# The first two modulation vectors of layer 0 from column slabs, with the projection of x two tiles behind

## The chip, the cores and the metric

The kernel runs on one core of a Trainium2 chip. The metric is the device time of one execution in microseconds (us). A core has a matrix engine (PE; the loading of its stationary operand is shown as PEld), a vector engine (DVE), an activation engine (ACT), GpSimd (POOL), a queue that issues most DMAs (SP), and 16 DMA engines that all queues share. Each engine works its instructions off in the order in which the build put them, and waits where an instruction's inputs are not there yet.

## The reference

A two-layer transformer block on x (512 tokens x 1024) with a context (256 tokens x 1024). Each layer is modulated by six vectors of 1024 that come from a matrix product with the conditioning vectors; the first two of layer 0 (shift `sh1`, scale `sc1`) are what the first projection waits for. Everything is float32.

```
mod  = silu(c)     @ ada_w[l] + ada_b[l]        # 1024 -> 6 * 1024
modc = silu(c_ctx) @ ada_w[l] + ada_b[l]
sh1, sc1, g1, sh2, sc2, g2 = split(mod, 6)      # likewise csh1 ... of modc
a  = rmsnorm(h,  norm1_g[l]) * (1 + sc1)  + sh1
ac = rmsnorm(hc, norm1_g[l]) * (1 + csc1) + csh1
y, yc = even_mixer(a, ac, ...)   # layer 0: q, k, v, u projections, attention, gated MLP
h = h + g1 * y ; h = h + g2 * swiglu(modulate(h, ...)) ; the same for hc ; then layer 1
```

## The kernel before

All activations are kept transposed: tile k of x (`hx[k]`) holds features 128k to 128k+127 in the partitions and the 512 tokens in the columns; there are 8 tiles. A float32 product is done as three matmuls (`mm3`, lines 100 to 102): each operand is split into a rounded part (hi) and a rest (lo), and hi x hi, hi x lo and lo x hi are summed in PSUM. For a weight block (`unit`) the raw block is loaded by SP (line 72), ACT makes hi (line 75), POOL makes lo (line 78). There are five raw buffers, and six weight slots plus three of a tag `wq`.

The start of `even()` is what the change is about. In the kernel before it goes like this:

- x (2 MB) is loaded in four pieces. ACT squares each tile and DVE adds the squares up (`squares`, lines 185 and 187); a matmul with ones sums over partitions (line 150), DVE makes 1/rms (lines 129 to 133) and a diagonal of it (line 167), and a matmul with ones (`spread`, line 177) puts 1/rms of each token in all partitions of a PSUM bank.
- The modulation vectors: `ada_load` (line 344) loads two row blocks of one vector's 1024 columns in 1 MB, into four buffers (tag `ar`). `ada_step` (line 351) multiplies the 32-column conditioning block `cst[:, k, :]` with row block k, four column quarters into four partition groups of one PSUM bank; the sum over all eight row blocks must be complete before any of the vector is known. `ada_out` copies the bank to SBUF (line 358), transposes it (line 360) and adds the bias and the gain (lines 364 and 368). The scale is done first, then the shift: 4 MB of weights each.
- `warm` (line 376) puts matmuls without use between the steps, two behind each step of the scale, three behind each step of the shift and six at the end.
- When the scale is there, DVE multiplies all eight tiles by scale and 1/rms (line 394). When the shift is there, ACT adds it and makes hi (line 457), DVE makes lo (line 458). Only then do the x products of the first half of the q and k columns begin: for each tile k, four column groups n, 96 matmuls of 512 columns in all into two PSUM pairs (`pw`).
- Then `modulate` does the same for the context tiles (lines 193 to 195), and the context products (96 matmuls of 256 columns, into `pb`) follow; `evacuate` (line 437) copies the x products out, and `rope` (lines 245 to 248, DVE and POOL) rotates them.
- The four other vectors of layer 0 (`ada_ahead`, `ada_some`, 16 loads of 1 MB, two vectors together) go between the products until well into the v projection.

The second half of the q and k columns, the v projection, attention and the rest of the kernel come behind that. The order within an engine's queue is fixed by a scheduler at build time, with priorities from the program's order; `issue_after` holds a load back until another DMA has been issued.

Of the kernel before, what the change touches and what calls it, by code (L numbers as in the profile page):

```python
# [14 lines left out]
P = 128  # L15
D = 1024
# [10 lines left out]
class Builder:  # L27
# [286 lines left out]
    def even(self):  # L314
        tc, nc, a = self.tc, self.nc, self.a
        self.open_ring(512, 5, 6)
        self.adap = tc.alloc_tile_pool(name="ada0", bufs=1, side="left", reuse_waits="tile")
        self.ropep = tc.alloc_tile_pool(name="rope0", bufs=1, side="left", reuse_waits="tile")
# [13 lines left out]
        self.ident = self.load(p0, a["ident"], [P, P], "ident")  # L332
# [6 lines left out]
        def ada_load(j, n, k):  # L339

            m = 2 // n
            t = self.adap.tile([P, m, n * D], F32, name=self.uid("ar"), tag="ar", bufs=4)
            src = a["ada0"][k * P:(k + m) * P, j * D:(j + n) * D].rearrange("(k p) c -> p k c", p=P)
            self.last_slab = nc.sync.dma_start(t, src)
            return [t[:, i, :] for i in range(m)]
# [8 lines left out]
        def ada_out(j, n, ps, pt):  # L354

            row = self.tmp("t")
            nb = 2 * n
            nc.scalar.copy(row[:, :nb * P], ps[:, :nb * P])
            for b in range(nb):
                nc.tensor.transpose(pt[:, b * P:(b + 1) * P], row[:, b * P:(b + 1) * P], self.ident)  # L360
            v = pt[:, :nb * P].rearrange("p (b q w) -> p q b w", b=nb, q=4)
            q = lambda t: t[:, j * KT:(j + n) * KT].rearrange("p (q b) -> p q b", q=4)
            for who in range(2):
                nc.vector.tensor_tensor(q(self.mod[who]), v[:, :, :, who], q(self.adab), ALU.add)
                for i in range(j, j + n):
                    if i in (1, 4):
                        m = self.mod[who][:, i * KT:(i + 1) * KT]
                        nc.vector.scalar_tensor_tensor(m, m, 1.0, self.gain(i // 3, 0), ALU.add, ALU.mult)
            return row
# [9 lines left out]
        slabs = sum([ada_load(1, 1, k) for k in range(0, KT, 2)], [])  # L379
        self.adab = self.load(p0, a["ada_b"], [P, 96], "adab")  # L380
        self.gains = self.load(p0, a["gains"], [P, 5 * KT], "gains")
        rd = self.rstd_diag([(sq, TX)], 1.0 / D)[0]
        ps0 = self.fill()
        for k in range(KT):
            ada_step(ps0, k, slabs[k])
            if k % 2:
                slabs += ada_load(0, 1, k - 1)
            if k == 3:
                rx = self.spread(rd)
            warm(slabs[k][:, :P], 2)  # L390
        scaled = self.bank()
        ada_out(1, 1, ps0, scaled)
        for k in range(KT):
            nc.vector.scalar_tensor_tensor(hx[k], hx[k], self.modcol(0, 1, k, 0), rx, ALU.mult, ALU.mult)
        ps0 = self.fill()
        for k in range(KT):
            ada_step(ps0, k, slabs[KT + k])
# [11 lines left out]
        def ada_ahead(n):  # L409
            for _ in range(min(n, len(rest))):  # L410
                j, k = rest.pop(0)
                loaded.append((j, k, ada_load(j, 2, k)[0]))
# [26 lines left out]
        with tc.issue_after(self.last_slab.ins):  # L439
            ctx_load()  # L440
        for half, heads in enumerate(((0, 1), (2, 3))):
            w2 = [self.wide(), self.wide()]
            accx = [w[:, h * 512:(h + 1) * 512] for w in w2 for h in range(2)]
            W = []
            for k in range(KT):
                t = self.adap.tile([P, 2, 512], F32R, name=self.uid("wq"), tag="wq", bufs=3) if k % 3 == 2 else None
                with tc.issue_after(self.last_slab.ins) if half == 0 else ExitStack():
                    W.append(self.blocks(a["qk"][half, k], 512, t=t))
                    if half == 0:
                        if k > 4:  # L450
                            with tc.issue_after(self.last_w.ins):
                                ada_ahead(1)
                        if k == 7:
                            tabs += [self.load(self.ropep, a[n], [P, TX], n) for n in ("cos", "sin")]
                if half == 0:
                    t, sh = hx[k], self.modcol(0, 0, k, 0)
                    nc.scalar.activation(axx[k][0], t, AF.Identity, bias=sh)
                    nc.vector.scalar_tensor_tensor(axx[k][1], t, sh, axx[k][0].bitcast(F32), ALU.add, ALU.subtract)  # L458
                elif k % 2:
                    ada_ahead(1)  # L460
                    ada_some()
                for n in range(4):
                    self.mm3(accx[n], W[k][n], axx[k], k == 0, k == KT - 1)
                if half == 0 and k == 4:
                    rd = self.rstd_diag([(self.squares(hc, TC), TC)], 1.0 / D)[0]
                if half == 0 and k == 5:
                    rc = self.spread(rd)
                    for i in range(KT):
                        self.modulate(hc[i], TC, self.modcol(0, 1, i, 1), self.modcol(0, 0, i, 1), rc, axc[i])
# [863 lines left out]
def prep(inp):  # L1333
# [12 lines left out]
    r["ada0"] = c(A["ada_w"][0])  # L1346
# [57 lines left out]
```

## Time and profile before

| what | value |
|---|---|
| runs of the kernel before | 1641.31, 1640.96, 1637.72 us; median 1640.96 |
| the profiled execution, first to last instruction (its span) | 1641.9 us |
| PE busy, share of the span | 1542.8 us, 94% |
| DVE, ACT, POOL busy | 65%, 44%, 47% |
| DMA queue of SP, share of 16 engines | 28.4% |
| mean granted clock of PE | 0.977 |

The page gives for the profiled execution its span alone; a time of its own beside it is not listed. The span lies 0.6 to 4.2 us above the three runs. A row of the timeline reads: start in us, duration, engine, line, operation, output<-inputs, shapes, count, and in brackets how long the engine sat idle before and what released it. A row of the windows reads: from:to, length, busy time (and instructions) of PE, PEld, DVE, ACT and POOL, the granted clock of PE, the busy share of the DMA engines, and GB/s.

### The profile page before, as it was taken

To read this page: it belongs to the slowest core of one execution; us is meant where nothing else is said; L and a number is where in the kernel's file an instruction comes from. 1 tells how busy PE (TensorE), PEld (TensorE's weight loads), DVE (VectorE), ACT (ScalarE), POOL (GpSimd) and SP (SyncE) were. 2 spreads that over 40 slices of the span, in tenths; PEclk is the share of its full clock that TensorE was granted. 3 is DMA by queue.
4 is the path that set the end of the run, shared out by engine and by line. 5 is a ranking of instruction groups with operands and counts; after the bars stand their busy time and mean duration, and the time that the engine had idled before them with its cause. 6 is when DMAs were issued, how large, how long until landed. Compare 5 with 4: busy or idle time off the path is not lost.

```text
span 1641.9 us, 24642 instructions
## 1 busy us (share of the span) xinstructions
PE 1542.8 (94%) x9547; PEld 1367.1 (83%) x9547; DVE 1073.0 (65%) x1980; ACT 724.5 (44%) x1472; POOL 766.9 (47%) x543
## 2 busy tenths in 40 slices
PE   6999989999999999999999988999989999999996
PEld 4776877899899889998989978777868989898886
DVE  4621788756857788666665585665667857666665
ACT  2423675645533233333333244555664544444443
POOL 0463221062157666666666316532222466675662
PEclk9999989999999999999999999999999999999998
DMA  8744100141223343343432012110233222322201
GB/s 317 298 153 169 40 7 1 65 139 68 76 79 116 105 139 131 105 150 126 142 131 77 27 51 91 52 33 25 74 116 123 65 103 92 101 90 103 90 27 52
DMA packets 47957, 161.98 MB, mean 99 GB/s; under 512 B 5472, under 2 KB 9952, under 8 KB 40160
## 3 DMA queue, kind: packets, MB, share of 16 engines
q1 hardware_dynamic: 47696, 160.28, 28.4%
q8 instruction: 75, 1.23, 0.3%
q14 instruction: 42, 0.34, 0.1%
q10 hardware_dynamic: 144, 0.13, 0.0%
HBM read 158.29 MB, written 2.10 MB: 98 GB/s over the span
## 4 chain that ended last, share of the span: by engine, by line
PE 69%; DVE 11%; POOL 6%; DMA 5%; ACT 4%; issue 3%; POOLq 0%; SPq 0%; DVEq 0%; ACTq 0%
PE pw L100 9%; PE pw L101 9%; PE pw L102 9%; PE pb L100 7%; PE pb L101 7%; PE pb L102 7%; POOL w L917 5%; DMA raw<-ffn_in 3%; PE pf L100 3%; PE pf L101 2%; PE pf L102 2%; PE pb L1257 2%; PE pb L1246 2%; PE pf L351 2%; DVE t L968 2%
## 5 line engine op out<-in xcount | busy, mean ns | idle before, releaser
L100 PE MATMUL pw<-ax,w 128*128 128x384 f32 (+2 forms) x732 | 237.5, 328 | 16.1 <-DVE q L1012 6.7
L101 PE MATMUL pw<-ax,w 128*128 128x384 f32 (+2 forms) x732 | 237.9, 325 | 4.1 <-DVE ax L458 2.5
L78 POOL TENSOR_TENSOR w<-raw,w 128x512 fp32r<-128x512 f32 (+1 forms) x84 | 127.6, 1526 | 243.2 <-ACT w L75 220.8
L102 PE MATMUL pw<-ax,w 128*128 128x384 f32 (+2 forms) x732 | 236.7, 325 | 2.1 <-POOL w L917 2.1
L917 POOL TENSOR_TENSOR w<-raw,w 128x512 fp32r<-128x512 f32 x119 | 177.7, 1507 | 54.2 <-ACT w L913 53.4
L917 POOL TENSOR_TENSOR w<-t,w 128x512 fp32r<-128x512 f32 x90 | 133.4, 1482 | 139.9 <-ACT w L913 136.5
L100 PE MATMUL pb<-hh,w 128*128 128x512 f32 x480 | 167.3, 362 | 12.8 <-ACT hh L116 8.3
L766 DVE SCALAR_TENSOR_TENSOR xT<-pb,mod,xT 128x512 f32<-128x512 f32 (+3 forms) x208 | 144.5, 704 | 43.8 <-PE pb L102 43.1
L101 PE MATMUL pb<-hh,w 128*128 128x512 f32 x480 | 171.2, 358 | 0.5 <-POOL hh L117 0.5
L102 PE MATMUL pb<-hh,w 128*128 128x512 f32 x480 | 170.7, 357 | 0.0
L100 PEld LDWEIGHTS pw<-ax,w 128*128 128x128 f32 x732 | 142.0, 195 | 27.2 <-DVE q L1012 8.1
L100 PE MATMUL pw<-T,w 128*128 128x384 f32 (+1 forms) x508 | 159.1, 314 | 4.8 <-DVE hs L1008 2.4
L101 PE MATMUL pw<-T,w 128*128 128x384 f32 (+1 forms) x508 | 158.6, 312 | 4.0 <-DVE T L117 4.0
L102 PE MATMUL pw<-T,w 128*128 128x384 f32 (+1 forms) x508 | 158.2, 312 | 0.0
L101 PEld LDWEIGHTS pw<-ax,w 128*128 128x128 f32 x732 | 142.6, 195 | 12.1 <-DVE ax L458 3.4
L102 PEld LDWEIGHTS pw<-ax,w 128*128 128x128 f32 x732 | 142.4, 195 | 6.0 <-POOL w L917 2.7
L913 ACT CAST w<-t 128x512 fp32r<-128x512 f32 x104 | 64.5, 621 | 176.8 <-DVE t L968 122.5
L917 POOL TENSOR_TENSOR w<-rawo,w 128x512 fp32r<-128x512 f32 x63 | 94.1, 1493 | 66.5 <-ACT w L913 66.5
L100 PEld LDWEIGHTS pb<-hh,w 128*128 128x128 f32 x480 | 89.5, 189 | 27.0 <-ACT hh L116 10.8
L100 PEld LDWEIGHTS pw<-T,w 128*128 128x128 f32 x508 | 97.2, 192 | 9.7 <-DVE hs L1008 3.9
L101 PEld LDWEIGHTS pw<-T,w 128*128 128x128 f32 x508 | 97.4, 192 | 6.6 <-DVE T L117 4.6
L102 PEld LDWEIGHTS pb<-hh,w 128*128 128x128 f32 x480 | 90.3, 188 | 13.1
(363 smaller groups left out, 4056.7 us busy)
## 6 DMA issues: line engine op xcount, KB each, us to landing
raw<-ffn_in SPq DMA_DIRECT2D x44, 1024.0 KB, 4.9
ar<-ada SPq DMA_DIRECT2D x24, 1024.0 KB, 7.3
ar<-ada SPq DMA_DIRECT2D x48, 512.0 KB, 3.5
rawo<-ffn_out SPq DMA_DIRECT2D x44, 512.0 KB, 3.9
raw<-odd_out SPq DMA_DIRECT2D x32, 256.0 KB, 2.7
raw<-qk SPq DMA_DIRECT2D x16, 256.0 KB, 7.9
raw<-uv SPq DMA_DIRECT2D x16, 256.0 KB, 2.7
raw<-even_out SPq DMA_DIRECT2D x8, 512.0 KB, 4.2
```

The lines of the kernel that those rows point to most:

```text
L78: eng.tensor_tensor(lo, raw, hi.bitcast(F32), ALU.subtract)
L100: mm(out, s[0], m[0], start=start, stop=False, **kw)
L101: mm(out, s[0], m[1], start=False, stop=False, **kw)
L102: return mm(out, s[1], m[0], start=False, stop=stop, **kw)
L351: nc.tensor.matmul(ps[32 * q:32 * q + 32, :w], cst[:, k, :], t[:, w * q:w * q + w], start=k == 0, stop=k == KT - 1, skip_group_check=True)
L766: self.nc.vector.scalar_tensor_tensor(h, ps[:, r], self.modcol(l, j, m, who), h, ALU.mult, ALU.add)
L913: nc.scalar.copy(t[:, 0, :], src)
L917: eng.tensor_tensor(t[:, 1, :], src, t[:, 0, :].bitcast(F32), ALU.subtract)
L968: nc.vector.tensor_tensor(t, x, y, how)
L1246: last = nc.tensor.transpose(pt[:, x * P:(x + 1) * P], es[2 * (x % 2) + x // 2][:, kb * P:(kb + 1) * P], self.ident)
L1257: nc.tensor.matmul(po[64 * h:64 * h + 64, :], V[vb][:, 64 * g:64 * g + 64], t[:, h * TC:h * TC + TC], start=kb == 0, stop=kb == nb - 1, sk ...
```

## The change

The weights of the first two vectors are rearranged on the host: `ada_s[k]` is a slab of 1 MB that holds, for all eight row blocks, the 128 columns of tile k of the scale and of the shift. So one slab gives both vectors for one tile of x, and tile k can go on as soon as slab k is there. The parts:

- `slab` loads it (three `ar` buffers instead of four); `first_rows` does its eight matmuls (256 columns each) into four partition groups, two row blocks per group, and ACT copies the result to `row`; `first_cols` multiplies the two halves of `row` with `sel`, a 128 x 2 matrix of zeros and ones that sums the four groups and transposes at once; two DVE instructions add bias and gain.
- DVE multiplies each tile by 1/rms as soon as that is there (eight instructions, 128x512, 1/rms in PSUM), then applies scale and shift in one `tensor_scalar`; `split` makes hi on ACT and lo on DVE.
- In the loop over slabs the products of tile k-2 stand behind slab k's rows (`products(k - 2)`); the last two tiles' products stand behind the loop. The context's sum of squares is in the loop (k = 6), its modulation between the products of tiles 6 and 7.
- The q/k weight blocks are loaded between the slabs, the context behind slab 3; `ident`, `ada_b` and `gains` are loaded from ACT's queue, ahead of everything else there.
- `warm` is left behind the first three slabs, six times each; `ada_ahead(2)` and the rope tables come behind the loop.

```diff
-        self.ident = self.load(p0, a["ident"], [P, P], "ident")
+        self.ident = self.load(p0, a["ident"], [P, P], "ident", eng=nc.scalar)
+        self.adab = self.load(p0, a["ada_b"], [P, 96], "adab", eng=nc.scalar)
+        self.gains = self.load(p0, a["gains"], [P, 5 * KT], "gains", eng=nc.scalar)
...
+        def slab(k):
+            t = self.adap.tile([P, 2 * D], F32, name=self.uid("ar"), tag="ar", bufs=3)
+            self.last_slab = nc.sync.dma_start(t, a["ada_s"][k])
+            return t
+        def first_rows(t):
+            ps = self.fill()
+            for r in range(2):
+                for q in range(4):
+                    k = 4 * r + q
+                    nc.tensor.matmul(ps[32 * q:32 * q + 32, :2 * P], cst[:, k, :], t[:, 2 * P * k:2 * P * k + 2 * P],
+                                     start=r == 0, stop=r == 1, skip_group_check=True)
+            row = self.adap.tile([P, 2 * P], F32, name=self.uid("row"), tag="row", bufs=2)
+            nc.scalar.copy(row, ps[:, :2 * P])
+            return row
+        def first_cols(k, row):
+            pt = self.bank()
+            for n in range(2):
+                nc.tensor.matmul(pt[:, 2 * n:2 * n + 2], row[:, n * P:(n + 1) * P], sel, start=True, stop=True,
+                                 skip_group_check=True)
+            nc.vector.tensor_scalar(first[:, 0, k, :], pt[:, 0:2], one_b[:, k:k + 1], self.gain(0, 0)[:, k:k + 1],
+                                    ALU.add, ALU.mult)
+            nc.vector.tensor_scalar(first[:, 1, k, :], pt[:, 2:4], self.adab[:, k:k + 1], None, ALU.add)
...
-        ps0 = self.fill()
-        for k in range(KT):
-            ada_step(ps0, k, slabs[k])
...
-            warm(slabs[k][:, :P], 2)
...
-        for k in range(KT):
-            nc.vector.scalar_tensor_tensor(hx[k], hx[k], self.modcol(0, 1, k, 0), rx, ALU.mult, ALU.mult)
...
-            warm(slabs[KT + k][:, :P], 3)
-        row = ada_out(0, 1, ps0, scaled)
-        warm(row[:, :P], 6)
...
+                if half == 0:
+                    s = slab(k)
+                    rows[k] = first_rows(s)
+                    if k < 3:
+                        warm(s[:, :P], 6)
                 with tc.issue_after(self.last_slab.ins) if half == 0 else ExitStack():
                     W.append(self.blocks(a["qk"][half, k], 512, t=t))
...
+                    if half == 0 and k == 3:
+                        ctx_load()
                 if half == 0:
-                    t, sh = hx[k], self.modcol(0, 0, k, 0)
-                    nc.scalar.activation(axx[k][0], t, AF.Identity, bias=sh)
-                    nc.vector.scalar_tensor_tensor(axx[k][1], t, sh, axx[k][0].bitcast(F32), ALU.add, ALU.subtract)
+                    if k == 0:
+                        rx = self.spread(rd)
+                    for i in range(2 * k, 2 * k + 2) if k < 4 else ():
+                        nc.vector.tensor_tensor(hx[i], hx[i], rx, ALU.mult)
...
+                    if k > 1:
+                        products(k - 2)
+                    first_cols(k, rows.pop(k))
+                    nc.vector.tensor_scalar(hx[k], hx[k], first[:, 0, k, 0:1], first[:, 1, k, 0:1], ALU.mult, ALU.add)
+                    self.split(*axx[k], hx[k])
+                    if k == 6:
+                        rd = self.rstd_diag([(self.squares(hc, TC), TC)], 1.0 / D)[0]
+                    continue
...
+            if half == 0:
+                with tc.issue_after(self.last_w.ins):
+                    tabs += [self.load(self.ropep, a[n], [P, TX], n) for n in ("cos", "sin")]
+                    ada_ahead(2)
+                products(KT - 2)
+                rc = self.spread(rd)
+                for i in range(KT):
+                    self.modulate(hc[i], TC, first[:, 0, i, 1:2], first[:, 1, i, 1:2], rc, axc[i])
+                products(KT - 1)
```

More of the change, by code (lines that the diff above doesn't have):

```diff
@@ L364, in ada_out @@
                 nc.vector.tensor_tensor(q(self.mod[who]), v[:, :, :, who], q(self.adab), ALU.add)
[L365 to L369, printed above, removed]
+                if j == 4:
+                    m = self.mod[who][:, 4 * KT:5 * KT]
+                    nc.vector.scalar_tensor_tensor(m, m, 1.0, self.gain(1, 0), ALU.add, ALU.mult)
         idle = self.wide()
@@ L411, in ada_ahead @@
                 j, k = rest.pop(0)
-                loaded.append((j, k, ada_load(j, 2, k)[0]))
+                loaded.append((j, k, ada_load(j, k)))
         def ada_some():
@@ L460, in even @@
+                if k % 2:
                     ada_ahead(1)
                     ada_some()
[L462 to L469, printed above, removed]
+                products(k)
```

55 lines of the change are left out of this document (24 added, 31 removed).

## The prediction, made before the changed kernel had run

> **What bounds the kernel now.** I read first the page's shares and the windows of busy time cut at this start's stages, then the timeline and the chain of waits from 12 to 120 us. From the page, and the windows (from:to, length, busy PE, PEld, DVE, ACT, POOL, granted clock, DMA share, GB/s):
>
> ```profile
> span 1641.9 us, 24642 instructions
> ...
> PE 1542.8 (94%) x9547; PEld 1367.1 (83%) x9547; DVE 1073.0 (65%) x1980; ACT 724.5 (44%) x1472; POOL 766.9 (47%) x543
> ```
>
> ```profile
> 12.00:20.00 8.00, 8.00 (x54) 4.86 (x55) 2.67 (x15) 0.00 (x0) 0.00 (x0) 1.00 1.01 373
> ...
> 26.50:39.80 13.30, 12.97 (x126) 8.64 (x122) 7.99 (x19) 3.53 (x10) 0.50 (x1) 1.00 0.86 312
> 39.80:50.00 10.20, 7.31 (x30) 5.02 (x30) 10.13 (x9) 7.57 (x15) 9.55 (x7) 1.00 0.83 314
> 50.00:66.50 16.50, 16.50 (x83) 10.29 (x82) 8.40 (x26) 3.36 (x6) 2.89 (x2) 1.00 0.67 247
> ...
> 78.50:160.00 81.50, 81.50 (x458) 59.37 (x457) 15.48 (x28) 20.05 (x37) 43.91 (x32) 1.00 0.47 164
> 160.00:330.00 170.00, 156.14 (x934) 134.67 (x932) 135.20 (x353) 112.98 (x226) 24.35 (x15) 0.95 0.08 27
> ```
>
> From 50 us to 160 PE is never idle, over the whole span it is busy 94%, and the DMA engines have room behind 78 us (share 0.47, then 0.08). So what is won ahead of 50 us stays won. Until 39.8 us PE looks busy too, but with steps on slabs and matmuls of no use, while the DMA engines run full; from 39.8 to 50 us DVE is the full one (10.13 of 10.20) and PE waits. The reader is to see that the first useful product is the row to watch, and how much of the products is done at a later point:
>
> ```profile
> 39.89 0.73 PE L100 MATMUL pw<-ax,w 128*128 128x512 f32 x2 [0.42 <-ACT ax L457]
> 42.60 0.50 PE L101 MATMUL pw<-ax,w 128*128 128x512 f32 x1 [1.98 <-DVE ax L458]
> ...
> 54.09 0.50 PE L101 MATMUL pw<-ax,w 128*128 128x512 f32 x1
> ...
> 62.01 0.59 PE L177 MATMUL pb<-q,ones 128*128 128x256 f32 x2
> ...
> 66.55 0.50 PE L100 MATMUL pb<-ax,w 128*128 128x256 f32 x2
> ```
>
> Between 54.09 and 62.01 lie 34 products of 512 columns: 0.233 us each, 2.8 us a tile. At 66.55 the context products begin. By the order in which the build queues PE's instructions, 22 of the 96 x products are still to do then (10 of tile 6, all of tile 7), and the steps of four later slabs are done. In the changed order all 96 x products and three such slabs stand ahead of the first context product. The price of a later slab is in the chain of waits:
>
> ```profile
> 91.56 0.99 PE pf L351 x8
> ```
>
> So the point to compare with is 66.55 + 22 x 0.233 - 1.0 = **70.7 us**. I now work out when the changed kernel reaches it.
>
> **The change, part by part.** 1. *Until 1/rms is there.* The squares and the sum over partitions stay as they are, and so does the first step's start. Rows of the timeline, then of the chain of waits:
>
> ```profile
> 11.93 2.05 PE L150 MATMUL pb<-ones,sq 128*128 128x128 f32 x8 [11.93 <-DVE sq L187]
> 13.91 1.08 PE L351 MATMUL pf<-ar,cst 128*32 128x256 f32 x8
> ...
> 37.97 1.50 PE L376 MATMUL pw<-t,ones 128*128 128x128 f32 x12
> ```
>
> ```profile
> 13.98 1.01 PE pf L351 x8
> 14.99 1.16 PE pw L376 x4
> ...
> 18.02 0.57 PE pf L351 x8
> ...
> 20.45 0.86 PE pb L177 x2
> ```
>
> A float32 matmul has two records, so a slab's eight matmuls are 16 records: 2.0 us at the first rate, 1.14 at the later one (0.57 for 8). All slabs together cost the same 64 matmuls as before. Six warm-ups are 12 records, 1.5 us at the later rate, some 2.2 here (4 records took 1.16 at the first rate, and the rows show the later one by 18.0). So: rows of slab 0 from 13.9 to 15.9, warm-ups to 18.1; slab 1's rows to 19.25, warm-ups to 20.75, `spread` to 21.6. Slab 0 was there at 13.9 before, and each slab with a weight block is 1.31 MB, 3.5 us at 373 GB/s: slabs 1 and 2 come by 17.4 and 20.9 at the latest, before PE wants them (18.1, 22.5). The three small loads on ACT's queue cost three issues, ahead of the first square, where ACT waits for x anyway.
>
> 2. *DVE, the bound from here.* It multiplies eight tiles by 1/rms out of PSUM; line 394 is the same shape. Then come the small vectors, scale and shift, and lo. Timeline rows and groups:
>
> ```profile
> 16.19 0.87 DVE L167 TENSOR_SCALAR q<-ident,sm 128x128 f32<-128x128 f32 x4
> ...
> 26.88 5.35 DVE L394 SCALAR_TENSOR_TENSOR hx<-hx,mod,pb 128x512 f32<-128x512 f32 x8
> ...
> 38.32 0.42 DVE L187 TENSOR_TENSOR sq<-sq,q 128x256 f32<-128x256 f32 x1
> ```
>
> ```profile
> L187 DVE TENSOR_TENSOR sq<-sq,q 128x512 f32<-128x512 f32 x4 | 2.8, 692 | 6.6 <-ACT q L185 6.3
> ```
>
> DVE's queue up to the first lo: eight by 1/rms 5.35; eight small ones at 0.2 (from 0.87 for four) 1.6, and `subg` 0.2; `tensor_scalar` on 128x512 for tiles 0 to 3; one context square 0.42; lo 0.69. No row shows that `tensor_scalar`: between 0.22 (a quarter of the columns, line 167) and 0.74 (line 458 undisturbed, below); I take 0.45, the middle, four times 1.8. Sum 10.1, from 21.7: the first lo is there at **31.8**, and as two products of hi stand ahead of it, the products begin as if at 31.3. The Trainium skill, "VectorE: DVE Perf Modes", Mode 2x_2P, says that such an instruction with float32 from SBUF makes two results per cycle; by it, half of line 187's 0.69 each as an estimate, all would come 0.4 us earlier. No run here shows it yet.
>
> PE's queue holds slab 2's rows (22.5 to 23.6, warm-ups to 25.1), slab 3's rows and the columns of slabs 2 and 3 ahead of the first product, so the product of tile 0 stands behind three further slabs and not two. Slab 3's buffer is free at 18.1; a 1 MB slab landed 5.3 us after its issue at the least:
>
> ```profile
> DMA to landing us min/median/max: 5.3/8.1/14.1
> ```
>
> that is 23.4, in time. ACT's queue holds four context squares ahead of tile 0's hi; the context's first half is issued behind slab 3 and block 3 and lands by 20.9 + 1.83 MB at 373 GB/s = 25.8, while ACT gets slab 3's rows to copy only at 26.3. So DVE, not the DMA, sets 31.3.
>
> 3. *From 31.3 PE is the bound.* Its queue up to the first context product: 96 products 22.4; rows of slabs 4 to 7, 4 x 1.14 = 4.6; their columns, eight matmuls of two columns; the context's sum and `spread` 0.9 (a quarter of line 150's row, with half the records at twice the rate, and half of line 177's 0.86); three later slabs 3.0. A column matmul has no row of its own; the bounds are 0.1, half a transpose, and 0.22, a whole one (0.44 for two):
>
> ```profile
> 118.79 0.44 PE pb L360 x4
> ```
>
> I take 0.16, 1.3 in all. Sum 32.2; 31.3 + 32.2 = 63.5. The warm-ups removed (28 of 46) lie ahead of the first product in both kernels and cost or save nothing by themselves.
>
> 4. *The clock.* PE has little to do from 26.3, when slab 3's rows are done, to 31.8, and nothing that warms. Windows and timeline of attention show what a gap can do:
>
> ```profile
> 230.00:240.00 10.00, 7.35 (x31) 6.38 (x32) 8.40 (x28) 8.94 (x16) 0.00 (x0) 0.66 0.00 0
> ```
>
> ```profile
> 233.10 0.58 PE L535 MATMUL pw<-kh,qb 128*128 128x256 f32 x1 [2.54 <-ACT e L538]
> ...
> 239.63 0.28 PE L535 MATMUL pw<-kl,qb 128*128 128x256 f32 x1
> ```
>
> After 2.54 us of idling PE ran some 6.2 us at about half rate, 3.1 lost; after the 1.98 us at 42.60 it lost nothing (clock 1.00 in that window). Bounds 0 and 3.1; the gap here is long but broken by columns and two products, so I take 2.0: 65.5. The Trainium skill, "TensorE: Matmul & The Clock Gate", Part 1, says that the clock falls to half after an idle window of about 3.4 us and needs as long a busy one to come back; it speaks against taking the warm-ups away. By it the loss here would be about 1.7 us (half of 3.4, an estimate) if the gap fills a window, and the end 65.2. The row agrees in the factor, not in the 3.4: 2.54 us were enough there, and 6.2 went by.
>
> 5. *The context products behind it.* DVE now rotates q and k (rope) while it modulates the context; before, the rope came at 78 us. Groups of the first 220 us, two rows for one instruction with and without POOL at work:
>
> ```profile
> L458 DVE SCALAR_TENSOR_TENSOR ax<-hx,mod,ax 128x512 fp32r<-128x512 f32 x8 | 10.1, 1269 | 0.0
> ...
> L246 DVE TENSOR_TENSOR f<-f,cos 128x512 f32<-128x512 f32 x8 | 7.3, 908 | 0.2
> ...
> L245 DVE STREAM_SHUFFLE sh<-f 128x512 f32<-128x512 f32 x8 | 6.0, 746 | 0.0
> ...
> L195 DVE SCALAR_TENSOR_TENSOR ax<-t,mod,ax 128x256 fp32r<-128x256 f32 x8 | 4.5, 572 | 0.6 <-ACT ax L194 0.4
> ...
> L193 DVE SCALAR_TENSOR_TENSOR t<-hc,mod,pb 128x256 f32<-128x256 f32 x8 | 3.7, 476 | 7.7 <-PE pb L177 7.7
> ```
>
> ```profile
> 40.78 1.77 DVE L458 SCALAR_TENSOR_TENSOR ax<-hx,mod,ax 128x512 fp32r<-128x512 f32 x1
> ...
> 50.25 0.74 DVE L458 SCALAR_TENSOR_TENSOR ax<-hx,mod,ax 128x512 fp32r<-128x512 f32 x1
> ```
>
> Four rotations 4 x (0.91 + 0.75) = 6.6 and eight tiles 8 x (0.48 + 0.57) = 8.4 are 15.0 us. They begin behind `spread`, two slab steps and tile 7's products, about 4.7 us ahead of the first context product, with some 1.3 of waiting for copies; so the last tile's lo comes about 11.5 after it, where PE wants it at about 11.3. I take a stall of 0.5, from 0 to 3 (if the twelve instructions with two SBUF inputs go as in the disturbed row, 1.77 for 0.74). End 66.0.
>
> So 70.7 - 66.0 = **4.7 us** are won. The later slabs are loaded in time: of the three ahead of the context, the first is issued when slab 5's buffer is free (47 us) and wanted ten later. Three buffers instead of four then hold SP back behind each later slab until PE has used the one three before it, and weight blocks wait behind it; DMA shares of 0.47 and less say that this has cover. In attention and at the start of layer 1's FFN the order of a few dozen PE instructions changes; PE idles 14 us from 160 to 330, so a shift of 2 us either way goes into the range. The span becomes 1641.9 - 4.7 = 1637.2; taken from the median of the runs, 1640.96 - 4.7 = **1636.3**.
>
> **The rivals.** *Slower, by ACT's queue.* ACT's order holds the cast of weight block 7 ahead of the copy of slab 5's rows, and behind that hi of tile 4. Slab 7 is issued only when PE has used slab 4's, after tile 1's products: 31.3 + 2.0 + 5.6 + 1.1 = 40.0; block 7 is issued 0.4 later. PE wants slab 5's columns at 47.1. The raw blocks of the first 60 us:
>
> ```profile
> DMA to landing us min/median/max: 2.5/7.9/11.7
> ```
>
> ```profile
> 25.58 0.37 ACT L358 COPY t<-pf 128x256 f32<-128x256 f32 x1 [15.16 <-PE pf L351]
> ...
> 40.05 0.60 ACT L75 CAST w<-raw 128x512 fp32r<-128x512 f32 x1
> ```
>
> With the least landing (slab 5.3, block 0.7 behind it) it is 46.0 + 0.6 + 0.4 = 47.0, just in time. With 11.7 it is 53.1: 6.0 of stall and a clock that falls again, 3.1: 4.4 slower than now, **1645.4**. It decides from block 7 landing at about 49, 3 us late. For it: PE, SP and ACT wait for one another in a ring; against it: SP's queue is empty then. *Nearly no change, by the clock.* It falls fully at the start (3.1) and once more at a wait for rows or columns (3.1): 4.7 + 2.0 - 6.2 = 0.5 faster, **1640.5**. For it: 28 warm-ups gone, the row at 233.10; against it: from 31.8 PE's queue is dense. *Faster by more.* No fall of the clock (2.0), no stall in the context (0.5), `tensor_scalar` at 0.22 and columns at 0.1 (0.9 and 0.5), and the shift in attention to the good side (1.5): 10.1 faster, **1630.9**. The change does rearrange what it says; only the two tiles are three on PE.
>
> **How the numbers follow.** Forecast 0.55, with 2.5 to 7 us won by the clock's and the context's bounds (1634 to 1638.5); faster by more 0.13; nearly no change 0.15; slower 0.17. This kernel's measurement can tell about 0.2%, 3.3 us, from no change. Of the forecast 0.43 lies beyond that; with 0.13, faster is 0.56. Same: 0.12 of the forecast and 0.12 of the clock's rival, 0.24. Slower: 0.17 and the clock's rival's bad end, 0.03: 0.20. The range holds forecast and clock, most of the faster case and that part of the slower one in which block 7 is up to 7 us late: 1630.5 to 1644.5.
>
> **What would show it.** In the profile after: first product with lo at 31 to 32 us (before 42.60); context products from about 66 us with no x products left; DVE full from 21 to 32; eight `tensor_scalar` of 128x512 at 0.2 to 0.7; the granted clock in 30 to 40 between 0.7 and 1.0. Wrong it would be by a PE wait for slab 5's columns or tile 4's hi with ACT at block 7's cast, by a first lo after 36 us, or by PE idling between 66 and 160 us.

## The result: slower by 0.3 to 0.6%, and where the forecast 4.7 us went

In its first four runs the changed kernel took 1650.24 us (median; 1648.93 to 1650.76) beside 1639.47 us before: ratio 1.0059, interval 1.0042 to 1.0075. Twelve later runs gave 1646.27 us (1639.33 to 1652.44) beside 1641.84: ratio 1.0030, interval 1.0013 to 1.0047. So it is 4 to 11 us slower, where 4.7 us faster was forecast. The profiled execution has a span of 1649.0 us and a time of 1650.76 us.

From the page after: the span, and the engines' shares, which tell nothing (PE has 1.4 us less to do in 7 us more).

```profile
span 1649.0 us, 24622 instructions
...
PE 1541.4 (93%) x9519; PEld 1367.2 (83%) x9519; DVE 1077.0 (65%) x2000; ACT 726.8 (44%) x1478; POOL 770.3 (47%) x543
```

The timeline of PE after, at the two points that the forecast named and behind them:

```profile
13.17 2.04 PE L150 MATMUL pb<-ones,sq 128*128 128x128 f32 x8 [13.17 <-DVE sq L187]
...
29.10 0.73 PE L100 MATMUL pw<-ax,w 128*128 128x512 f32 x2 [0.82 <-ACT ax L116]
...
31.38 0.79 PE L101 MATMUL pw<-ax,w 128*128 128x512 f32 x1 [1.54 <-DVE ax L117]
...
66.08 0.51 PE L100 MATMUL pb<-ax,w 128*128 128x256 f32 x2
...
73.20 1.04 PE L386 MATMUL pf<-ar,cst 128*32 128x512 f32 x2
...
77.63 0.38 PE L100 MATMUL pb<-ax,w 128*128 128x256 f32 x1 [0.55 <-ACT ax L194]
...
79.35 0.58 PE L101 MATMUL pb<-ax,w 128*128 128x256 f32 x1 [1.33 <-DVE ax L195]
...
82.44 0.44 PE L101 MATMUL pb<-ax,w 128*128 128x256 f32 x1 [0.17 <-DVE ax L195]
...
85.85 1.06 PE L386 MATMUL pf<-ar,cst 128*32 128x512 f32 x6
```

The first product with lo stands at 31.38 us (before: 42.60) and the context products begin at 66.08, where the comparable point of before was 70.7: the 4.6 us are won. Then PE waits three times, 2.05 us in all, and one step on a later slab is torn into one quarter (x2) and three (x6), which take 1.0 us each, as much as a whole one (x8). The chain of waits after says whose work sets this stretch:

```profile
64.39 0.36 DVE t L193
...
66.55 2.90 DVE ax L195 x2
69.45 0.72 DVE sh L245
...
72.77 2.18 DVE ax L195 x2
74.95 1.70 DVE f L246
...
80.97 1.43 DVE ax L195
82.44 0.44 PE pb L101
...
119.79 0.44 PE pb L395 x4
```

From 64.4 to 82.4 us the chain runs through DVE alone: the context's scale (L193) and lo (L195) with the rotation (L245, L246) between them. The last row, the transposes of the first later vector, is a milestone that every kernel here has, with the same products and steps ahead of it but for the warm-ups; before it stands at 118.79. So by 120 us the changed kernel is 1.0 us *behind*: 4.6 won, 5.6 lost. The windows after, then the one of before for the same stretch:

```profile
21.70:31.40 9.70, 6.83 (x65) 4.66 (x63) 9.02 (x24) 5.53 (x13) 1.84 (x2) 1.00 1.03 389
...
31.40:34.81 3.41, 3.41 (x8) 2.73 (x9) 3.38 (x7) 1.48 (x4) 1.95 (x1) 0.50 1.04 421
...
66.00:80.00 14.00, 12.12 (x86) 10.34 (x83) 14.00 (x19) 5.43 (x11) 12.90 (x9) 0.97 0.40 129
...
79.20:82.61 3.41, 3.10 (x13) 2.80 (x14) 3.19 (x3) 0.47 (x1) 3.41 (x3) 0.50 0.56 151
...
1321.60:1328.43 6.83, 6.14 (x28) 6.14 (x29) 3.38 (x7) 2.54 (x5) 4.54 (x4) 0.50 0.14 46
```

```profile
66.00:80.00 14.00, 14.00 (x96) 12.54 (x93) 9.60 (x22) 7.84 (x16) 5.08 (x4) 1.00 0.91 362
```

DVE is full (14.00 of 14.00) and POOL nearly (12.90, before 5.08); the waits cost a stretch of half clock as well (79.20 to 82.61). The rest of the 7 us between the two spans comes behind: in the same DVE row the pair stands 8.0 us apart at 1334 us, of which a half-clock stretch of 6.83 us at 1321.60, which before lacks, makes 3.4. The row in before, after, and a later profile of the changed kernel, which lacks that stretch and stands 5.0 us behind before:

```profile
1334.24 1.76 DVE L968 TENSOR_TENSOR t<-raw,t 128x512 f32<-128x512 f32 x1 [1.19 <-POOL w L917]
```

```profile
1342.23 1.76 DVE L997 TENSOR_TENSOR t<-raw,t 128x512 f32<-128x512 f32 x1 [0.53 <-POOL w L946]
```

```profile
1339.27 1.77 DVE L997 TENSOR_TENSOR t<-raw,t 128x512 f32<-128x512 f32 x1 [0.52 <-POOL w L946]
```

### The profile page after: what moved, and what is told of

It reads as the page before. It is cut to its first block, busy times and chain, and to the rows that moved or that the text cites. A ratio compares the mean times of both kernels' runs of the same rounds, so it can differ in the third digit from the quotient of the medians.

```text
span 1649.0 us, 24622 instructions
## 1 busy us (share of the span) xinstructions
PE 1541.4 (93%) x9519; PEld 1367.2 (83%) x9519; DVE 1077.0 (65%) x2000; ACT 726.8 (44%) x1478; POOL 770.3 (47%) x543
## 4 chain that ended last, share of the span: by engine, by line
PE 64%; DVE 14%; POOL 7%; DMA 6%; ACT 5%; issue 4%; POOLq 0%; SPq 0%; ACTq 0%; DVEq 0%
PE pw L100 8%; PE pw L101 8%; PE pw L102 8%; PE pb L100 7%; PE pb L101 7%; PE pb L102 7%; POOL w L946 5%; DMA raw<-ffn_in 4%; PE pf L100 3%; PE pf L101 2%; PE pf L102 2%; PE pb L1286 2%; PE pb L1275 2%; DVE t L997 2%; ACT w L942 1%
## 5 line engine op out<-in xcount | busy, mean ns | idle before, releaser
L100 PEld LDWEIGHTS pw<-ax,w 128*128 128x128 f32 x732 | 143.5, 197 | 30.0 <-DVE q L1041 9.1
L101 PEld LDWEIGHTS pw<-ax,w 128*128 128x128 f32 x732 | 144.3, 197 | 12.0 <-DVE ax L195 3.6
L102 PEld LDWEIGHTS pw<-ax,w 128*128 128x128 f32 x732 | 144.2, 197 | 6.1 <-POOL w L946 2.6
L946 POOL TENSOR_TENSOR w<-rawo,w 128x512 fp32r<-128x512 f32 x63 | 94.7, 1502 | 65.5 <-ACT w L942 65.5
L100 PEld LDWEIGHTS pb<-hh,w 128*128 128x128 f32 x480 | 89.5, 189 | 28.9 <-ACT hh L116 11.9
L100 PE MATMUL pf<-ax,w 128*128 128x256 f32 (+2 forms) x268 | 94.1, 351 | 8.5 <-DVE qf L246 5.7
```

The costliest lines, as they stand in the source:

```text
L100: mm(out, s[0], m[0], start=start, stop=False, **kw)
L101: mm(out, s[0], m[1], start=False, stop=False, **kw)
L102: return mm(out, s[1], m[0], start=False, stop=stop, **kw)
L946: eng.tensor_tensor(t[:, 1, :], src, t[:, 0, :].bitcast(F32), ALU.subtract)
```

## The experiments

My first theory had two parts: the context stretch (rotation ahead of the context's lo), and the order that the build writes for layer 1's FFN, which differs between before and after though the change touches neither. The rival: the new start itself, with its buffers and loads, costs later. Times are medians; each group of runs had its own runs of before, and "against before" is the difference of the medians; a bracket behind a ratio is its 95% interval. Further small edits serve here as handles, since the build answers them with other orders far away.

**Before, with a different order of layer 1.** Two more warm-ups behind each of eight steps make the build write the changed kernel's order for the last 2600 PE instructions.

```diff
-            warm(slabs[k][:, :P], 2)
+            warm(slabs[k][:, :P], 4)
```

> The kernel before with four warm-ups instead of two behind each of its first eight steps. Its start, buffers and loads are those of before, but the order that the build then writes out for layer 1's FFN is the one of the changed kernel (the last 2600 PE instructions stand in the changed kernel's order). Theory (what is lost behind 1283 us comes from that order): the drift against before grows by 4 to 5 us between 1283 and 1331 us here too, with a wait of PE near 1321 and a fall of the clock to half for about 6.8 us behind it; in all 3 to 8 us slower than before, 1643 to 1648. Rival (the changed start, or its three buffers, costs later): no such step at 1283 to 1331, and at most 2 us slower than before, from the warm-ups.

1647.11 us against 1640.60: ratio 1.0037 (1.0023 to 1.0051). The total fits the theory, its place does not: 3.9 us are lost by the milestone (122.73). The first product stands 3.1 us later (42.96) behind the added warm-ups, and a half clock of 6.83 us follows from 45.15; this run does not separate the two. Between 1270 and 1331 us, along the DVE instructions that both kernels share, the drift grows by 1.0 us only (6.2 to 7.2; after: 3.1 to 8.0), with no fall of the clock between 1283 and 1331.

**Nine warm-ups behind the first three slabs.** This brings layer 1's FFN back to the order of before.

```diff
-                        warm(s[:, :P], 6)
+                        warm(s[:, :P], 9)
```

> The changed kernel with nine warm-ups instead of six behind each of the first three slabs. The start does the same work in the same pattern, and the order of layer 1's FFN is again that of the kernel before. Theory (order): the step of +5 at 1283 to 1331 us is gone, the rest of the drift stays, so 4 to 6 us faster than the changed kernel, 1644 to 1646. Rival (start): the loss at 1283 to 1331 stays, and the time is that of the changed kernel within 2 us, 1649 to 1651.

1636.29 us against 1640.60: ratio 0.9968 (0.9949 to 0.9986), far more than either theory gave. The milestone stands at 115.02, 4.8 us sooner than after: no half clock at 31 us, and in this order the context's products come later, behind slab steps, so that PE does not wait for lo although the rotation is still ahead of it. That has a price too: one later slab's step is torn into four quarters (66.69, 69.29, 71.89 and 77.13 us), 1.04 us each. Two causes changed at once, so the next pairs separate them.

**The rotation held back**, in the changed kernel, until the context's last lo is written. Behind the context PE's order is the changed kernel's, instruction for instruction.

```diff
-        nc.vector.scalar_tensor_tensor(out[1], t, sh, out[0].bitcast(F32), ALU.add, ALU.subtract)
+        self.last_lo = nc.vector.scalar_tensor_tensor(out[1], t, sh, out[0].bitcast(F32), ALU.add, ALU.subtract)
...
-                    self.rope(qk[n][:, :TX], qk[n][:, :TX], tabs)
+                    with tc.issue_after(self.last_lo.ins) if half == 0 else ExitStack():
+                        self.rope(qk[n][:, :TX], qk[n][:, :TX], tabs)
```

> The changed kernel with the rotation of q and k in the first half held back until the last lo of the context is written. The order of layer 1's FFN stays that of the changed kernel. Theory (the rotation ahead of the context's lo on DVE, and GpSimd's share of it beside it, cost the three waits of 2.05 us, the clock's 1.7 and the split step's 1.0 between 66 and 110 us): the context products run without waits, at about 108 us the kernel is 2.5 to 4.6 us ahead of before instead of 0.9 behind, and it ends 3 to 5 us faster than the changed kernel, 1645 to 1647; the step of +5 at 1283 to 1331 stays. Rival (the loss there is DMA or the later slabs' buffers): the waits at 77 to 83 us stay, or others take their place.

1640.42 us against 1640.60: ratio 1.0000 (0.9984 to 1.0017). That is below the 1645 to 1647 of the theory, which was reckoned from the first four runs. The milestone in its chain of waits, and the slab step, whole again, in its timeline:

```profile
113.58 0.44 PE pb L395 x4
```

```profile
79.62 1.06 PE L386 MATMUL pf<-ar,cst 128*32 128x512 f32 x8
```

PE waits nowhere between 60 and 112 us; the milestone comes 6.2 us sooner than after. Of these 0.8 stand already at the first product with lo (30.59), since x landed sooner in this execution; 5.4 are the context's. The step behind 1283 us did not stay at +5: here the drift grows by 2.3 between 1281 and 1331 us, in PE's order of the changed kernel.

**The same with the small loads moved** (identity on SP's queue, the other two behind the squares in the source). Their place turned out to be worth nothing that shows, but the build answers with another order in three stretches of layer 1, some 200 of 9061 PE instructions, and nowhere else.

```diff
-        self.ident = self.load(p0, a["ident"], [P, P], "ident", eng=nc.scalar)
-        self.adab = self.load(p0, a["ada_b"], [P, 96], "adab", eng=nc.scalar)
-        self.gains = self.load(p0, a["gains"], [P, 5 * KT], "gains", eng=nc.scalar)
+        self.ident = self.load(p0, a["ident"], [P, P], "ident")
...
+        sq = self.squares(hx, TX)
+        self.adab = self.load(p0, a["ada_b"], [P, 96], "adab", eng=nc.scalar)
+        self.gains = self.load(p0, a["gains"], [P, 5 * KT], "gains", eng=nc.scalar)
...
-        sq = self.squares(hx, TX)
```

> The same with the identity loaded from SP's queue again, behind x, and the two other small loads put behind the squares in the source; the order of layer 1's FFN is that of the kernel before. Theory (both causes): x lands up to 1 us sooner than in the changed kernel, the context runs without waits, and the step at 1283 to 1331 us is gone: 8 to 10 us faster than the changed kernel, 1640 to 1642, within 2 us of before or a little faster. Rival (each loss is replaced by another): 1645 or more.

1635.88 us against 1640.60: ratio 0.9965 (0.9949 to 0.9982), below the 1640 to 1642 of the theory. The milestone stands at 113.46.

**The other half of the square:** the changed kernel again, and the changed kernel with only the small loads moved.

> The changed kernel itself, so that it shares a chip and the runs of before with the next three. If the 1650.2 of its four runs is its own time: 1648 to 1652. If those four stood high in the clock's scatter (single runs of the other kernels scatter by 10 us): 1644 to 1647.

1646.27 against 1641.84, the 1.0030 of the first section. That is inside the second expectation: the first four runs stood high. In this execution the first context product comes at 65.22, and the milestone and the window of half clock are

```profile
120.73 0.44 PE pb L395 x4
```

```profile
78.30:85.13 6.83, 5.98 (x25) 5.59 (x26) 3.73 (x3) 1.57 (x5) 6.83 (x6) 0.50 0.26 77
```

so the clock stayed low for twice as long here as in the first profile (6.83 us for 3.41).

> The changed kernel with the identity on SP's queue behind x and the two small loads behind the squares in the source; the rotation stays where the change has it. Its order on PE differs from the changed kernel's only in three short stretches of layer 1 (some 200 of 9061 instructions), which stand as in the kernel before. Theory (layer 1's order costs 3 to 5 us by itself): at 108 us it is 0 to 1 us behind before, as the changed kernel is, and it ends 3 to 6 us faster than the changed kernel. Rival (what is lost behind 110 us is chance of the clock or the context's late effects): within 2 us of the changed kernel.

1641.73 against 1641.84: ratio 0.9994 (0.9975 to 1.0013), 4.5 us faster than the changed kernel as the theory says, with the milestone at 120.28, 1.5 us behind before. Against before, in us, each with an interval of about 3 us either way:

| | rotation as changed | rotation held back |
|---|---|---|
| layer 1 in the changed kernel's order | +4.4 | -0.2 |
| the three stretches in the other order | -0.1 | -4.7 |

Within these intervals the two effects add: 4.6 us for the rotation in either row, 4.5 for the order in either column. That the last cell is the forecast's -4.7 is luck: the next paragraph shows that part of the second effect is not the changed kernel's loss.

Where do the 4.5 sit? Mostly behind the first of the three stretches (983 to 989 us; the others lie in the FFN, at 1288 to 1304 and 1331 to 1339). PE's timeline of before, just behind it, then that of the run with the small loads moved:

```profile
1014.04 0.55 PE L100 MATMUL pf<-ax,w 128*128 128x512 f32 x1 [2.61 <-DVE qf L246]
...
1022.93 0.50 PE L100 MATMUL pf<-ax,w 128*128 128x512 f32 x1 [0.97 <-DVE qf L246]
```

```profile
1016.37 0.47 PE L100 MATMUL pf<-ax,w 128*128 128x512 f32 x1 [2.61 <-DVE qf L246]
...
1023.66 0.50 PE L100 MATMUL pf<-ax,w 128*128 128x512 f32 x1 [0.98 <-DVE qf L246]
```

8.9 us between the two waits in the one, 7.3 in the other; by 1060 us, along the DVE instructions that the kernels share, the other order has won 2.8 us against before, and so it has in the two runs above that have it too. In all fourteen profiles this goes together: in the ten with the slow order a step of half clock follows the first wait (1.7 us), in the four with the other order none does. But *before* has the slow order there, as the changed kernel has: the 2.8 are a gift of the other order, not a loss of the change. What is left for the FFN is under 2 us: that part of my theory, with its 4 to 5, fell.

**Nine warm-ups and the rotation held back.**

> The changed kernel with the rotation of the first half held back until the context's last lo is written, and nine warm-ups instead of six behind each of the first three slabs; layer 1's FFN stands in the order of the kernel before. Theory (context, the clock's fall at 31 us and layer 1's order add up): no fall of the clock at 30 us, at 108 us 6 to 8 us ahead of before, 1631 to 1634 in all. Rival (nine warm-ups and the rotation's place mend the same loss): at 108 us 4 to 5.5 us ahead, 1635 to 1637.

1634.68 us against 1641.84: ratio 0.9952 (0.9937 to 0.9967), milestone at 111.37, 7.4 us ahead of before. So the clock's fall at 31 us and the context do add, as the theory had it; the total lay just between the two expectations. Of the 3.65 us by which the milestone comes sooner than with nine warm-ups alone, 3.1 are the torn step, which stands whole here (73.46).

**Nine warm-ups and the small loads moved** (e6 is the run above with only the small loads moved).

> The changed kernel with nine warm-ups behind each of the first three slabs and the small loads as in e6; layer 1's FFN stands in the changed kernel's order, and the context's products are queued a little differently from the run with nine warm-ups alone. Theory (layer 1's order): 3 to 5 us slower than nine warm-ups alone, 1639 to 1642, with the loss behind 1000 us. Rival (chance or context): 1635 to 1637.5.

1640.04 us against 1641.84: ratio 0.9990 (0.9975 to 1.0005), though the milestone (114.60) is not later than with nine warm-ups alone. That is the time that the theory gave, and the 2.5 us between the two, against before, fit the stretch at 985 us, which is in the slow order here and in the fast one there. They do not show it by themselves: the two orders also differ near 235, from 458 to 514 and in the FFN, and the profiled executions, single ones, have spans of 1635.4 and 1636.9.

**Ten, eight and seven warm-ups, with the rotation held back** (one number each in the edit above). Ten brings the fast order at 985 us; eight and seven have layer 1 wholly in the changed kernel's order.

> The changed kernel with the rotation held back and ten warm-ups behind each of the first three slabs. Against the run with nine, PE's order differs behind the start only in some 40 products of layer 1 near 1010 us, which stand here as in the two runs that gained 2.8 us there. Theory (that stretch is worth 2.8 us, with or without the rest): no clock window near 1010 us, 2 to 3.5 us faster than with nine warm-ups, 1631 to 1633. Rival (the gain there is given back by later falls of the clock): 1633.5 to 1636.

1631.61 us against 1641.25: ratio 0.9942 (0.9930 to 0.9954), from five runs. 3.1 us faster than with nine, 2.5 by the differences against before, as the theory of that stretch says; the two intervals overlap, though. This is the best version tried: 9.6 us faster than before.

> The changed kernel with the rotation held back and eight warm-ups behind each of the first three slabs; layer 1 stands wholly in the changed kernel's order. Theory (the warm-ups keep the clock up at 31 us, which is worth 1.7, and the FFN's order of layer 1 costs 1 to 1.5): 1 to 2 us faster than with six warm-ups, 1638 to 1640. Rival (that FFN's order costs 4 us or more): beyond what stands ahead at 110 us it loses 4 us or more between 1270 and 1340.

1634.09 us against 1641.25: ratio 0.9954 (0.9937 to 0.9971). Both expectations missed: 7.0 us faster, against before, than with six, with the milestone at 114.02, no sooner. It has the changed kernel's order in layer 1's FFN and loses nothing there, which ends the FFN theory.

> The changed kernel with the rotation held back and seven warm-ups behind each of the first three slabs. Its PE order is that of the run with six warm-ups and the rotation held back, instruction for instruction, apart from the three warm-ups; the run with eight differs from it in some 200 products between 240 and 560 us and near 1230 us, and was 7 us faster though it stood no further ahead at 108 us. Theory (that order costs it): at 108 us 4.5 to 5.5 us ahead of before, and 1639 to 1642 in all, as with six. Rival (the clock's scatter made the run with six look slow): 1634 to 1637.

1638.30 us against 1640.46: ratio 0.9989 (0.9978 to 1.0001), the order of the run with six. It lies between the expectations, and its interval does not meet that of eight. So most of the difference goes with the order of some 200 products, which by the trace lie, but for ten ahead of the milestone, at 231 to 234, 457 to 512 and 1234 to 1236 us. Along the shared DVE instructions the profile with eight stands ahead of that with seven by 0.1 us at 200 us, 1.3 at 1200 and 4.1 at 1283, which points to the third place; with one execution of each it is not shown.

**The rotation without GpSimd's part.** In the changed kernel, sin product and sum of the first half are left out.

```diff
-        nc.gpsimd.tensor_tensor(sh, sh, tabs[1], ALU.mult)
-        nc.gpsimd.tensor_tensor(out, out, sh, ALU.add)
+        if add:
+            nc.gpsimd.tensor_tensor(sh, sh, tabs[1], ALU.mult)
+            nc.gpsimd.tensor_tensor(out, out, sh, ALU.add)
```

> The changed kernel without GpSimd's two instructions of each rotation of the first half (sin product and sum are left out); DVE still has the shuffles and cos products between the context's scale and lo, in nearly the changed kernel's order. Theory A (GpSimd beside DVE slows DVE's two-input instructions): lo falls from 1.1 to 1.5 us to 0.6 or less where GpSimd rests, the three waits of PE at 77 to 83 us shrink from 2 us to under 0.7, no clock window there, and at 108 us it is 3 to 5 us ahead of the changed kernel. Theory B (DVE's order alone, the rotation standing ahead of lo): the waits stay at 1.5 us or more and at 108 us it gains under 1.5.

1641.62 against 1641.25: ratio 1.0004 (0.9989 to 1.0018). The milestone stands at 115.58, 4.2 us sooner than after, and PE waits nowhere between 60 and 112 us, although DVE's order is nearly the same: theory A. The slab step is torn here too (74.94 and 81.64), so that is the order that the build wrote and not an effect of the waits. The groups of lo between 60 and 110 us, after and then here:

```profile
L195 DVE SCALAR_TENSOR_TENSOR ax<-t,first,ax 128x256 fp32r<-128x256 f32 x8 | 8.9, 1146 | 0.0
```

```profile
L195 DVE SCALAR_TENSOR_TENSOR ax<-t,first,ax 128x256 fp32r<-128x256 f32 x8 | 5.6, 739 | 0.2 <-ACT ax L194 0.2
```

And single rows of this run, of DVE and of POOL:

```profile
66.49 0.87 DVE L195 SCALAR_TENSOR_TENSOR ax<-t,first,ax 128x256 fp32r<-128x256 f32 x2
...
71.96 2.94 DVE L195 SCALAR_TENSOR_TENSOR ax<-t,first,ax 128x256 fp32r<-128x256 f32 x2
```

```profile
71.44 1.75 POOL L78 TENSOR_TENSOR wq<-raw,wq 128x512 fp32r<-128x512 f32 x1
73.14 1.48 POOL L78 TENSOR_TENSOR w<-raw,w 128x512 fp32r<-128x512 f32 x1
```

Two of them take 0.87 us while POOL rests and 2.94 beside POOL's weight blocks. The context's scale (L193), one of whose inputs lies in PSUM, takes 0.85 to 0.87 for two in either case. The Trainium skill, "SBUF — State Buffer", Who interferes with whom, says that a DVE instruction with two SBUF inputs contends with a GpSimd instruction that reads SBUF, because its second input comes through the read interface that they share. The rows agree: each lo took about as long as the POOL instruction beside it.

## Why the prediction failed, by its steps

**1. Rows and warm-ups: right in kind.** x landed 1.2 us later than in before's profile (line 150 at 13.17 for 11.93), but its first square stood at anything from 0.4 to 1.1 us later in the other runs of the changed start (5.46 to 6.16 for 5.10), with the small loads ahead or not; this looks like a scatter of the loads more than a price of the three issues, which no pair of runs here separates.

**2. DVE as the bound, 31.8: right** (31.38 for the products), but closer than its parts, which is luck: DVE began at 22.38 where 21.7 was worked out, and needed 9.0 us where 10.1 were summed. Two of the parts, in the group view after:

```profile
L474 DVE TENSOR_TENSOR hx<-hx,pb 128x512 f32<-128x512 f32 x8 | 4.9, 681 | 4.1 <-PE pb L177 4.1
...
L481 DVE TENSOR_SCALAR hx<-hx,first 128x512 f32<-128x512 f32 x8 | 4.2, 540 | 0.1
```

4.9 for 5.35, and 0.54 for the unseen `tensor_scalar` where 0.45 was taken (from its start to the next instruction's, 27.86 to 28.31 us, it is 0.45). The estimate of 0.35 by the Trainium skill, "VectorE: DVE Perf Modes", Mode 2x_2P, was too low; whether the mode was at work no run shows.

**3 and 4. PE from 31.3 and the clock: right**, 66.08 for 65.5 without step 5, with some luck. From the first product with lo PE needed 33.0 us besides the clock's loss where 31.7 were summed; the earlier start (0.4) and the clock (0.3) made up for half of that. One half-clock stretch of 3.41 us cost 1.7 where 2.0 was taken; in three other executions with six or seven warm-ups it lasted 6.83. Ten or nine warm-ups avoid it, eight and fewer did not.

**5. The context's stall: the step that failed.** It took 0.5, from 0 to 3. Measured from the first context product to the milestone, over the same work in the same order or nearly so, it is 5.3 to 7.1:

| kernel | first context product | milestone | between |
|---|---|---|---|
| changed | 66.08 | 119.79 | 53.7 |
| changed, later profile | 65.22 | 120.73 | 55.5 |
| changed, without GpSimd's part of the rotation | 66.00 | 115.58 | 49.6 |
| rotation held back (six, seven or eight warm-ups; small loads moved) | 65.05 to 65.72 | 113.46 to 114.13 | 48.4 in all four |

In the first profile the 5.3 are 2.05 of waits, 1.7 of half clock (79.20 to 82.61), 1.0 for the torn slab step and 0.5 that I can't assign; in the later one the clock took 3.4. Without GpSimd's part little more than the torn step is left, so the waits and the fall of the clock came from GpSimd's part. The step summed DVE's 15.0 us with the quiet rows, lo at 0.57 and cos at 0.91, though it had just moved POOL's part of the rotation beside them; after, lo took 1.15. The disturbed row (1.77 for 0.74) that it quoted for the bad end was the one to take. And a stall of 2 us brought a fall of the clock, and the order that the build wrote a torn step: neither was in the bound.

**Behind 120 us: a shift of 2 us either way was too narrow.** Median against before, less the milestone's difference, is what a kernel gains or loses behind the milestone: +2.5 us for the changed kernel (1646.27 and the later profile; +3.4 by the first profile's milestone), and between -2.5 (ten warm-ups) and +5.0 (six, rotation held back) for the others, none of which touches anything there. It follows the build's order in part: the four with the fast order at 985 us lie between -2.5 and +0.6; of the other eight seven lie between +0.3 and +5.0, and one, eight warm-ups, at -2.4. So of the 9.1 us between -4.7 and +4.4, 6.6 stood at the milestone by the later profile (5.7 by the first), nearly all of them the context's, and 2.5 (3.4) came behind it. That the order has a part in these the pair of eight and seven warm-ups shows (-2.4 and +2.5 at the same milestone); how they divide between order and clock stays open. The first four runs lie within the 1639 to 1652 of the twelve later ones, in their upper half; why is not known.

**The rivals.** ACT's queue was as tight as worked out and held: the cast of block 7 began at 45.64 us after 5.18 us of waiting for its load, and PE did not wait. The clock's rival had a second fall right, but behind waits for the context's lo and not for a slab's columns. "PE idling between 66 and 160 us" was the sign of failure named, and it is what came.

## What to carry to other kernels

Price a stage that moves beside another with the rows of both engines at work: here a DVE instruction with two SBUF inputs took about as long as the GpSimd instruction beside it (lo 1.1 to 1.5 us beside 1.3 to 1.8; 0.44 alone). When work is pulled forward, ask which later work now shares its engine, and hold that back. Where a scheduler orders the whole program, a change at the start also redraws orders far behind it; compare several neighbours of a version before a gain or loss of 0.3% is put down to the idea, and remember that the best of many is partly chosen for its luck.

## What the runs showed of the hardware

All half-clock stretches of one execution lie on one grid. After, they start at 31.4, 79.2, 232.8 and 1321.6 among others: the last three 14, 59 and 378 steps of 3.413 us from the first, and each lasts a whole number of steps, but for the last one, which the end of the span cuts. In all fourteen profiles the starts fit such a grid to a few hundredths of a step, and where it lies differs from one execution to the next. So one and the same wait can be cheap or dear. Before, and with ten warm-ups, each the PE row, the grid's step or steps that hold the wait, and the window behind:

```profile
557.74 1.44 PE L100 MATMUL pb<-hh,w 128*128 128x512 f32 x3 [2.86 <-ACT hh L116]
```

```profile
553.48:556.89 3.41, 1.40 (x9) 1.08 (x7) 3.16 (x5) 0.03 (x1) 2.33 (x2) 1.00 0.56 231
...
556.90:563.70 6.80, 5.96 (x18) 5.77 (x19) 1.64 (x4) 2.28 (x4) 3.13 (x2) 0.50 0.23 77
```

```profile
552.90 0.85 PE L100 MATMUL pb<-hh,w 128*128 128x512 f32 x3 [2.87 <-ACT hh L116]
```

```profile
548.36:551.77 3.41, 1.68 (x10) 1.35 (x8) 2.81 (x4) 0.28 (x1) 2.61 (x2) 1.00 0.77 317
551.77:555.18 3.41, 2.28 (x13) 2.19 (x14) 1.36 (x3) 1.73 (x3) 2.25 (x2) 1.00 0.28 58
...
552.90:559.70 6.80, 6.80 (x38) 6.54 (x39) 3.97 (x10) 1.98 (x4) 5.31 (x3) 1.00 0.26 77
```

2.86 us of waiting cost half the clock for 6.8 us in the one, 2.87 nothing in the other. What differs is how much of the wait falls into one step: PE idled 2.01 of 3.41 us (busy 1.40) in the one, 1.73 and then 1.13 in the other. Counted over all steps of the fourteen profiles, from 20 us to shortly before the last matmul, by PE's matmul records: of 188 falls of the clock 176 came behind a full step in which PE idled 1.7 us or more, the others behind 0.84 to 1.69, and no full step with more than 1.88 us of idling was followed by a full one. A half step was followed by full clock in the 178 cases in which PE idled at most 0.46 us in it, and by another half one in the 60 in which it idled 0.55 or more. So in these traces about half a step of idling drops the clock, and a nearly busy step brings it back.

An execution has 17 to 24 steps of half clock, 3.4 to 4 of them at its very end, where PE has little left to do; each of the others loses up to 1.7 us. That is where I see most of the 8 to 13 us by which twelve runs of one kernel differ: of the later runs of the changed kernel the two fastest (1639.33 and 1641.07) had granted clocks of 0.980 and 0.981, the two slowest (1650.22 and 1652.44) 0.974 and 0.973, and 0.007 of the time is 11.5 us. One execution of each kernel was profiled, two of the changed kernel, so a difference of a few us between two profiles proves nothing by itself. The Trainium skill, "TensorE: Matmul & The Clock Gate", Part 1, says that the window is free-running and 3413 ns long; the grid agrees. Its idle window of about 3.4 us is not needed: about half of one was enough here.
